# The residual placed in PSUM ahead of the expert products, and the last norm read from PSUM

## The chip, the cores and the metric

The kernel runs on one core of a Trainium2 chip. The metric is the device time of one execution in microseconds. A run gives the median of several executions; beside it one execution is profiled, and its trace gives every instruction's start and length.

## The reference

It is one layer of a transformer encoder over 512 tokens of width 1024, in float32. Attention of two kinds gives a mixed update, and the first norm gives `h`. What matters here is the second half of the layer:

```python
h = layer_norm(DN_ALPHA * h + mix, ln1_g, ln1_b)
ffn = peer_ffn(h, peer_w_q, peer_sub_keys, peer_u, peer_v)
gate = sigmoid(h @ ple_gate_w + ple_gate_b)
h = layer_norm(DN_ALPHA * h + ffn + gate * (p @ ple_w), ln2_g, ln2_b)

def peer_ffn(x, ...):            # per chunk of 128 tokens
    # idx, g: 8 heads x 16 experts of 16384, chosen by the best key sums, and their softmax
    hpre = einsum('td,ted->te', x, u_table[idx])
    act = g * gelu(hpre)
    return einsum('te,ted->td', act, v_table[idx])

def layer_norm(x, g, b):
    mu = mean(x); var = mean(square(x - mu))
    return (x - mu) * rsqrt(var + LN_EPS) * g + b
```

The layer ends with the last `layer_norm`, over the sum of the scaled `h`, the gate's part and the experts' part. The first two of these are the residual below.

## The kernel before

The 512 tokens are four chunks of 128. Chunk 0 (`NGC` is 1) is worked by gathering: for each of its 128 chosen experts POOL gathers a row of `u` or `v` per token into a buffer `gat`, and VectorE takes the dot product (line 1393) or adds the weighted row to `base[0]` (line 1404). Chunks 1 to 3 (`NDC` is 3, 384 tokens) are worked densely: the 16384 experts are 128 blocks of 128, and for each block TensorE multiplies the block's activations of 384 tokens with the block's 128 rows of `v` into PSUM.

For the dense chunks the sums of all blocks stand in PSUM from the first block to the last: `acc[c][hf]`, three chunks by two halves of 512 columns, six banks. Every operand is split into a high and a low part by the helper `split`: ScalarE copies the source to the high part (a cast to fp32r), VectorE subtracts it from the source for the low part. A block's products are three per bank (high by high, high by low, low by high), so 18 of 128x512, in `expert_out` (line 1419). The very first product into a bank has `start=True`, which overwrites what the bank held.

The residual is `base[c]`: for chunk 0 a tile of its own, for chunks 1 to 3 the tile `h[c]` itself, which the gate's last step (line 1232) overwrites with the scaled `h` plus the gate's part. This is done well before the loop.

Before the loop, "lead blocks" make the inputs of 100 of the 128 blocks: eight products of `u` by the tokens (`whole`), into the PSUM tile `mm`, or `hp` for the last two; then ScalarE's Gelu takes the sums out. These blocks and the gate's products are steps of the generator `pe_work`, one product each, which earlier stages advance as TensorE has time. What is left of it when the loop is near is run out in a fixed block just ahead of the loop. `mm` and `tr` (the sums of the routing weights, copied by ScalarE into `g_st`, line 1055) lie in the six banks that `acc` takes over.

The loop over the blocks has VectorE and SyncE in the order of the program (`manual_schedule`); the other engines are ordered by the scheduler of the language. In iteration `n` SyncE loads the rows of `v`, the routing weights `gt` and the activations `ge`; VectorE multiplies the latter two (line 1468); the two splits follow, then the 18 products. In the first 28 iterations `expert_in` makes the remaining blocks' inputs, with a 512 KB load of `raw` (line 116). The steps of chunk 0's gathers are spread over the iterations. The products of the last four blocks (124 to 127) are held back and run bank by bank, so that the banks complete one after the other.

After the loop all engines are ordered by the scheduler. For each chunk 1 to 3 VectorE adds `acc` to `base` half by half with the row sums as a by-product (line 1500); the mean comes from these sums, ScalarE squares the centred row with its sum as a by-product (line 151), and after the square root VectorE takes the reciprocal, four small steps that refine it (`rsqrt_refine`, lines 129 to 132), a centring pass with the gain (line 159) and a scaling pass with the bias (line 160). One store of 512 KB per chunk follows. Chunk 0 takes its mean and variance by `bn_stats` over two halves of `base[0]` instead.

Of the kernel before, what the change touches and what calls it, by code (L numbers as in the profile page):

```python
# [9 lines left out]
F32 = mybir.dt.float32  # L10
# [5 lines left out]
OP = mybir.AluOpType  # L16
# [3 lines left out]
D = 1024  # L20
# [7 lines left out]
EPS = 1e-5  # L28
# [45 lines left out]
def tile_encoder_layer(ctx: ExitStack, tc: tile.TileContext, A: dict, out: bass.AP):  # L74
    nc = tc.nc
# [1305 lines left out]
    psA = ctx.enter_context(tc.tile_pool(name="psA", bufs=1, space=PSUM, reuse_waits="tile"))  # L1381
    acc = [[psA.tile([128, 512], F32, name=f"acc{c}{hf}") for hf in range(2)] for c in range(NDC)]
    scr = pG.tile([128, D], F32, name="scr")

    def fetch_u(c, k):
        u = pG.tile([128, D], F32, name="gat", bufs=GATS)
# [27 lines left out]
    def expert_out(x, c, halves=(0, 1)):  # L1414
        n, ah, al, vh, vl = x
        cs = slice(c * 128, (c + 1) * 128)
        for i, (a, b) in enumerate(((ah, vh), (ah, vl), (al, vh))):
            for hf in halves:
                nc.tensor.matmul(acc[c][hf], a[:, cs], b[:, hf * 512:(hf + 1) * 512],  # L1419
                                 start=(n == 0 and i == 0), stop=(n == 127 and i == 2))  # L1420

    steps = list(gather_steps())
    late = []
# [1 line left out]
    with tc.manual_schedule(engines={nc.vector.engine, nc.scalar.engine, nc.tensor.engine, nc.sync.engine,  # L1425
                                     nc.gpsimd.engine}):
        gating = True
        gt_next = first_g
        v_next = {n: load_v(n) for n in (2, 3, 4)}
        for _ in pe_work:  # L1430
            pass
    done, spent = PRE, 0
    with tc.manual_schedule(engines={nc.vector.engine, nc.sync.engine}):
        for n, i in enumerate(order):
            if n % GB == 0:
                gt = gt_next
            if n < 128 - GB:
                for q in range(4):
                    if n % GB == (GB // 2 - 1 + q if n < KEPT + 128 - LEAD + 4 else GB - 2 + q // 2):
                        gt_next = load_g(n // GB * GB + GB, 3 - q if n < GB else q, gt_next, q == 0)  # L1440
            if n not in v_cut:
                raw = v_next.pop(n, None) or load_v(n)
            if n in v_cut:
                vh, vl = v_cut[n]
                ah = pO.tile([128, N_D], F32R, name="a_hi")
                al = pO.tile([128, N_D], F32R, name="a_lo")
            elif n in (124, 125):
                vh = wst.tile([128, D], F32R, name="whi")
                vl = wst.tile([128, D], F32R, name="wlo")
                a2 = wst.tile([128, 2, N_D], F32R, name="raw", bufs=3)  # L1450
                ah, al = a2[:, 0], a2[:, 1]
            else:
                if in_wst(n):
                    vh = wst.tile([128, D], F32R, name="whi")
                    vl = wst.tile([128, D], F32R, name="wlo")
                else:
                    vh = pP.tile([128, D], F32R, name="v_hi")
                    vl = pP.tile([128, D], F32R, name="v_lo")
                ah = pO.tile([128, N_D], F32R, name="a_hi")
                al = pO.tile([128, N_D], F32R, name="a_lo")  # L1460
            if 0 <= n + GE_AHEAD - (128 - SPILL) < SPILL:
                ge = pB.tile([128, N_U], F32, name="ge", bufs=GES)
                nc.sync.dma_start(ge, ge_dram[order[n + GE_AHEAD]])
                ge_t[order[n + GE_AHEAD]] = ge
            ge = ge_t.pop(i)
            a = gt[:, :, n % GB, :]
            dn = gt[:, N_S // GT:, n % GB, :]
            nc.vector.tensor_tensor(dn, dn, ge.rearrange("p (g t) -> p g t", t=GT), op=OP.mult)  # L1468
            if n not in v_cut:
                split(vh, vl, raw)  # L1470
            split(ah.rearrange("p (g t) -> p g t", t=GT), al.rearrange("p (g t) -> p g t", t=GT), a)
            late.append((n, ah, al, vh, vl))
            if n < 124:
                for c in range(NDC):
                    expert_out(late[0], c)
                late = []
            u = block_of_u(n)
            if u:
                expert_in(u)
            if n >= NO_GATHER:  # L1480
                spent += 1 if u else LATE
            upto = min(len(steps), PRE + math.ceil((len(steps) - PRE) * spent / (128 - (1 - LATE) * LEAD - 3 - NO_GATHER)))
            for f in steps[done:upto]:
                f()
            done = upto
# [5 lines left out]

    lg = row_bcast(pG, A["ln2_g"], "gat", GATS)
    lb = row_bcast(pG, A["ln2_b"], "gat", GATS)
    for c in range(4):
        fsum = None
        if c >= NGC:
            fsum = small.tile([128, 2], F32, name="fsum", bufs=2)
            for hf in range(2):
                hs = slice(hf * 512, (hf + 1) * 512)
                nc.vector.scalar_tensor_tensor(base[c][:, hs], base[c][:, hs], 1.0, acc[c - NGC][hf], op0=OP.mult,  # L1500
                                               op1=OP.add, accum_out=fsum[:, hf:hf + 1])
        layer_norm(base[c], lg, lb, fsum, scr)
        nc.sync.dma_start(out[c * 128:(c + 1) * 128, :], base[c])


# [85 lines left out]
```

## Time and profile before

| | |
|---|---|
| median of 3 runs | 1518.24 us (1515.72, 1518.24, 1519.31) |
| profiled execution, its own time | 1514.74 us |
| its span in the trace | 1512.7 us, so 2.0 us lie around it |
| granted TensorE clock, mean | 0.997 |
| TensorE busy | 1481.9 us, 98% |
| VectorE busy | 1302.4 us, 86% |
| ScalarE busy | 657.6 us, 43% |
| POOL busy | 571.9 us, 38% |

The trace's times are microseconds from the start of the span. PE is TensorE (PEld its weight loads), DVE VectorE, ACT ScalarE, SP SyncE; a q behind the name is an engine's instruction queue. `out<-in` names the tiles that an instruction writes and reads, and xN counts merged instructions. `base[1]` to `base[3]` are named `h` in the trace.

### The profile page before, as it was taken

Reading aid. Unit: us, or ns where it says so; the run is one execution under the profiler, and the core shown is the slowest. Engines: PE = TensorE matmul, PEld = TensorE weight load, DVE = VectorE, ACT = ScalarE, POOL = GpSimd, SP = SyncE. Lnnn points to the kernel's source line nnn. Section 1 sums busy time; section 2 is a strip of 40 time slices with the busy share of each in tenths; the row PEclk is TensorE's granted clock in tenths of the full one; section 3 lists DMA queues with packets and bytes.
Section 4 is the critical chain, followed back from the end, with each engine's and each line's share of the span. In section 5 each row is a group of like instructions: output and inputs, shape, how many; then the busy total and the mean of one; then the engine's idle time right before and its main releaser. Section 6 shows DMA issues by size and latency. Waiting matters only on the chain.

```text
span 1512.7 us, 23117 instructions
## 1 busy us (share of the span) xinstructions
PE 1481.9 (98%) x7757; PEld 1255.0 (83%) x7757; DVE 1302.4 (86%) x3020; ACT 657.6 (43%) x1224; POOL 571.9 (38%) x520
## 2 busy tenths in 40 slices
PE   8999999999999999999999999999999999999997
PEld 5788767788888889888988987888888888888885
DVE  7376785679989999899888978999999999999996
ACT  3355785333222566212765643444334333334342
POOL 1013110010015333455532434565555766666620
PEclk9999999999999999999999999999999999999999
DMA  7343240142279999999999999999999999999981
GB/s 250 98 116 95 84 126 29 42 143 84 89 226 335 341 401 379 416 408 412 400 407 375 388 384 382 411 410 416 414 413 411 412 411 409 412 411 409 412 323 76
DMA packets 194360, 459.90 MB, mean 304 GB/s; under 512 B 18241, under 2 KB 97985, under 8 KB 192706
## 3 DMA queue, kind: packets, MB, share of 16 engines
q1 hardware_dynamic: 121856, 214.60, 38.6%
q0 software_dynamic: 57984, 207.12, 34.8%
q10 hardware_dynamic: 14402, 36.71, 6.3%
q8 instruction: 61, 1.00, 0.2%
q14 instruction: 57, 0.47, 0.1%
HBM read 414.59 MB, written 40.89 MB: 301 GB/s over the span
## 4 chain that ended last, share of the span: by engine, by line
PE 69%; DVE 15%; DMA 8%; issue 4%; ACT 3%; POOL 1%; SPq 0%; DVEq 0%; POOLq 0%; ACTq 0%
PE acc L1419 33%; PE mm L1185 4%; PE mm L123 3%; PE hp L1185 3%; DMA wlo<-in_u_rows_dram,s_ix 3%; PE mm L125 3%; PE mm L124 3%; PE pj L123 3%; PE pj L124 3%; DMA whi<-in_u_rows_dram,s_ix 3%; PE tr L1043 3%; PE pj L125 3%; DVE oh_j L1081 2%; PE hp L123 2%; PE hp L125 2%
## 5 line engine op out<-in xcount | busy, mean ns | idle before, releaser
L1402 POOL DMA_INDIRECT gat<-in_v_rows_dram,i_sel x128 | 214.1, 1673 | 117.9 <-DVE base L1404 96.6
L1185 PE MATMUL mm<-whole,raw 128*128 128x256 f32 x848 | 190.9, 379 | 0.0
L104 ACT CAST whi<-raw 128x1024 fp32r<-128x1024 f32 (+4 forms) x117 | 117.3, 1004 | 160.6 <-DMA raw<-in_v_rows_dram 44.7
L1387 POOL DMA_INDIRECT gat<-in_u_rows_dram,i_sel x102 | 131.5, 1289 | 118.2 <-DVE hdot L1393 75.5
L1185 PEld LDWEIGHTS mm<-whole,raw 128*128 128x128 f32 x848 | 158.8, 190 | 20.4
L104 DVE TENSOR_TENSOR wlo<-raw,whi 128x1024 fp32r<-128x1024 f32 (+4 forms) x117 | 136.0, 1163 | 34.8 <-ACT whi L104 34.6
L1404 DVE SCALAR_TENSOR_TENSOR base<-gat,hdot,base 128x1024 f32<-128x1024 f32 x128 | 163.8, 1280 | 1.6
L1419 PE MATMUL acc<-v_hi,a_hi 128*128 128x512 f32 x480 | 149.5, 392 | 3.4 <-ACT a_hi L104 3.4
L1419 PE MATMUL acc<-v_lo,a_hi 128*128 128x512 f32 x480 | 149.0, 390 | 0.0
L1419 PE MATMUL acc<-v_hi,a_lo 128*128 128x512 f32 x480 | 148.8, 390 | 0.0
L104 ACT CAST v_hi<-v_raw 128x1024 fp32r<-128x1024 f32 x80 | 84.1, 1051 | 116.7 <-issue 49.1
L104 ACT CAST a_hi<-gt 128x384 fp32r<-128x384 f32 x126 | 64.6, 513 | 158.4 <-DVE gt L1468 99.3
L1098 POOL DMA_INDIRECT whi<-in_u_rows_dram,s_ix x51 | 57.7, 1131 | 199.6 <-DVE cand L946 133.5
L1393 DVE CUSTOM_DVE_ANT_0 scr<-gat,h 128x1024 f32<-128x1024 f32 x102 | 124.6, 1222 | 2.3
L1081 DVE TENSOR_SCALAR oh_j<-iota,eT 128x128 f32<-128x128 f32 x384 | 114.6, 372 | 0.0
L1419 PEld LDWEIGHTS acc<-v_lo,a_hi 128*128 128x128 f32 x480 | 90.2, 188 | 19.4 <-DVE v_lo L104 0.3
L1419 PEld LDWEIGHTS acc<-v_hi,a_lo 128*128 128x128 f32 x480 | 90.4, 188 | 19.1
L1419 PEld LDWEIGHTS acc<-v_hi,a_hi 128*128 128x128 f32 x480 | 88.5, 189 | 20.8 <-ACT a_hi L104 4.3
L104 DVE TENSOR_TENSOR v_lo<-v_raw,v_hi 128x1024 fp32r<-128x1024 f32 x80 | 97.4, 1217 | 7.8 <-ACT v_hi L104 7.7
L1043 PEld LDWEIGHTS tr<-oh_i,oh_j 128*128 128x128 f32 x768 | 93.5, 192 | 9.4 <-ACT g_st L1055 4.3
L1043 PE MATMUL tr<-oh_i,oh_j 128*128 128x128 f32 x768 | 95.9, 277 | 3.9 <-DVE oh_j L1081 2.1
L1098 POOL DMA_INDIRECT wlo<-in_u_rows_dram,s_ix x51 | 63.0, 1235 | 86.1 <-DVE s_dot L1100 45.8
(391 smaller groups left out, 3492.9 us busy)
## 6 DMA issues: line engine op xcount, KB each, us to landing
raw<-in_uT_dram SPq DMA_DIRECT2D x103, 512.0 KB, 7.2
v_raw<-in_v_rows_dram SPq DMA_DIRECT2D x82, 512.0 KB, 10.7
g_dram<-g_st ACTq DMA_DIRECT2D x12, 2048.0 KB, 10.5
gt<-g_dram SPq DMA_DIRECT2D x60, 384.0 KB, 12.9
raw<-in_v_rows_dram SPq DMA_DIRECT2D x44, 512.0 KB, 12.5
raw_u<-in_uT_dram SPq DMA_DIRECT2D x25, 512.0 KB, 6.8
ge_dram<-ge ACTq DMA_DIRECT2D x88, 128.0 KB, 6.7
ge<-ge_dram SPq DMA_DIRECT2D x88, 128.0 KB, 12.1
```

The costliest lines, as they stand in the source:

```text
L104: cut = nc.scalar.copy(hi, src), nc.vector.tensor_tensor(lo, src, r32(hi), op=OP.subtract)
L123: nc.tensor.matmul(ps, a[0], b[0], start=start, stop=False)
L125: nc.tensor.matmul(ps, a[1], b[0], start=False, stop=stop)
L1043: nc.tensor.matmul(ps[:, i * 128:(i + 1) * 128], oj[:, 4 * r + i, :], oi[:, 4 * r + i, :], start=True, stop=True)
L1081: nc.vector.tensor_scalar(oj[:, i], iota, eT[:, 1, t0 + i:t0 + i + 1], eT[:, 2, t0 + i:t0 + i + 1], op0=OP.is_equal, op1=OP.mult)
L1098: nc.gpsimd.indirect_dma_start(out=u[:], out_offset=None, in_=u_rows, in_offset=bass.IndirectOffsetOnAxis(ap=ix[:, k:k + 1], axis=0))
L1185: nc.tensor.matmul(ps[:, :N_U], raw[:, k], whole[:, k, :], start=(k == 0), stop=(k == 7))
L1387: nc.gpsimd.indirect_dma_start(out=u[:], out_offset=None, in_=u_rows, in_offset=bass.IndirectOffsetOnAxis(ap=i_sel[:, c, k:k + 1], axis=0))
L1393: nc.vector.tensor_tensor_reduce(scr, u, h[c], op0=OP.mult, op1=OP.add, accum_out=hdot[:, c, k:k + 1], scale=1.0, scalar=0.0)
L1402: nc.gpsimd.indirect_dma_start(out=u[:], out_offset=None, in_=v_rows, in_offset=bass.IndirectOffsetOnAxis(ap=i_sel[:, c, k:k + 1], axis=0))
L1404: nc.vector.scalar_tensor_tensor(base[c], u, hdot[:, c, k:k + 1], base[c], op0=OP.mult, op1=OP.add)
L1419: nc.tensor.matmul(acc[c][hf], a[:, cs], b[:, hf * 512:(hf + 1) * 512], start=(n == 0 and i == 0), stop=(n == 127 and i == 2))
```

## The change

Ahead of the loop, in its fixed block, `pe_work` is advanced by eight steps; then for each of the six banks a product of two slices of `hTh` (the transposed `h`, with no use for its value) is written with `start=True`, and ScalarE copies the residual of that chunk and half over it. The rest of `pe_work` follows, and the loop's products all add to what stands in the bank. The casts to the high parts of block 0's activations and of block 2's rows of `v` are ordered behind the last of these copies.

Behind the loop, chunk 0 is normed as before. For chunks 1 to 3 VectorE and SyncE follow a written order: `bn_stats` of each half straight from PSUM, the aggregate, the centring from PSUM into `base` by halves, the scaling, and then the next chunk's first statistics. For the last chunk the second half is centred after the first half is scaled and stored, and then scaled and stored by itself.

```diff
@@ -1381,6 +1381,14 @@
     psA = ctx.enter_context(tc.tile_pool(name="psA", bufs=1, space=PSUM, reuse_waits="tile"))
     acc = [[psA.tile([128, 512], F32, name=f"acc{c}{hf}") for hf in range(2)] for c in range(NDC)]
     scr = pG.tile([128, D], F32, name="scr")
+    halves = [slice(hf * 512, (hf + 1) * 512) for hf in range(2)]
+
+    def open_sums():
+        for c in range(NDC):
+            for hf, hs in enumerate(halves):
+                nc.tensor.matmul(acc[c][hf], hTh[:, 0, 0:128], hTh[:, 0, :], start=True, stop=False)
+                last_copy = nc.scalar.copy(acc[c][hf], base[NGC + c][:, hs])
+        return last_copy
 
     def fetch_u(c, k):
         u = pG.tile([128, D], F32, name="gat", bufs=GATS)
@@ -1417,7 +1425,7 @@
         for i, (a, b) in enumerate(((ah, vh), (ah, vl), (al, vh))):
             for hf in halves:
                 nc.tensor.matmul(acc[c][hf], a[:, cs], b[:, hf * 512:(hf + 1) * 512],
-                                 start=(n == 0 and i == 0), stop=(n == 127 and i == 2))
+                                 start=False, stop=(n == 127 and i == 2))
 
     steps = list(gather_steps())
     late = []
@@ -1427,6 +1435,9 @@
         gating = True
         gt_next = first_g
         v_next = {n: load_v(n) for n in (2, 3, 4)}
+        for _ in range(8):
+            next(pe_work)
+        opened = open_sums()
         for _ in pe_work:
             pass
     done, spent = PRE, 0
@@ -1467,8 +1478,14 @@
             dn = gt[:, N_S // GT:, n % GB, :]
             nc.vector.tensor_tensor(dn, dn, ge.rearrange("p (g t) -> p g t", t=GT), op=OP.mult)
             if n not in v_cut:
+                if n == 2:
+                    turned.append(opened)
                 split(vh, vl, raw)
+                turned.clear()
+            if n == 0:
+                turned.append(opened)
             split(ah.rearrange("p (g t) -> p g t", t=GT), al.rearrange("p (g t) -> p g t", t=GT), a)
+            turned.clear()
             late.append((n, ah, al, vh, vl))
             if n < 124:
                 for c in range(NDC):
@@ -1491,16 +1508,48 @@
 
     lg = row_bcast(pG, A["ln2_g"], "gat", GATS)
     lb = row_bcast(pG, A["ln2_b"], "gat", GATS)
-    for c in range(4):
-        fsum = None
-        if c >= NGC:
-            fsum = small.tile([128, 2], F32, name="fsum", bufs=2)
-            for hf in range(2):
-                hs = slice(hf * 512, (hf + 1) * 512)
-                nc.vector.scalar_tensor_tensor(base[c][:, hs], base[c][:, hs], 1.0, acc[c - NGC][hf], op0=OP.mult,
-                                               op1=OP.add, accum_out=fsum[:, hf:hf + 1])
-        layer_norm(base[c], lg, lb, fsum, scr)
+    for c in range(NGC):
+        layer_norm(base[c], lg, lb)
         nc.sync.dma_start(out[c * 128:(c + 1) * 128, :], base[c])
+
+    stats = [small.tile([128, 2, 6], F32, name=f"st_{c}", bufs=1) for c in range(NDC)]
+
+    def stat(c, hf):
+        nc.vector.bn_stats(stats[c][:, hf, :], acc[c][hf])
+
+    with tc.manual_schedule(engines={nc.vector.engine, nc.sync.engine}):
+        stat(0, 0)
+        for c in range(NDC):
+            r = base[NGC + c]
+            o = out[(NGC + c) * 128:(NGC + c + 1) * 128]
+            ys = small.tile([128, 8], F32, name="ln_y")
+            mu = small.tile([128, 2], F32, name="ln_mu")
+            ve, sd, y0, y, t = (ys[:, i:i + 1] for i in range(5))
+
+            def centre(hf):
+                hs = halves[hf]
+                nc.vector.scalar_tensor_tensor(r[:, hs], acc[c][hf], mu[:, 0:1], lg[:, hs], op0=OP.subtract, op1=OP.mult)
+
+            def scale(hs):
+                nc.vector.scalar_tensor_tensor(r[:, hs], r[:, hs], y, lb[:, hs], op0=OP.mult, op1=OP.add)
+                nc.sync.dma_start(o[:, hs], r[:, hs])
+
+            stat(c, 1)
+            nc.vector.bn_aggr(mu, stats[c])
+            nc.vector.tensor_scalar(ve, mu[:, 1:2], EPS, None, op0=OP.add)
+            nc.scalar.sqrt(sd, ve)
+            centre(0)
+            if c < NDC - 1:
+                centre(1)
+            nc.vector.reciprocal(y0, sd)
+            rsqrt_refine(y, y0, ve, t)
+            if c < NDC - 1:
+                scale(slice(0, D))
+                stat(c + 1, 0)
+            else:
+                scale(halves[0])
+                centre(1)
+                scale(halves[1])
 
 
 # ---- launch: one core; host code only lays the arrays out ----
```

## Rows read from the trace of the kernel before

**Rows 1.** The page, part 1: busy time, share of the span, instructions.

```profile
PE 1481.9 (98%) x7757; PEld 1255.0 (83%) x7757; DVE 1302.4 (86%) x3020; ACT 657.6 (43%) x1224; POOL 571.9 (38%) x520
```

**Rows 2.** Chain of waits, 855 to 960 us: start, us, what.

```profile
893.89 12.30 PE acc L1419 x54
...
906.22 1.07 ACT v_hi L104
...
913.29 10.17 DMA raw<-in_uT_dram
```

**Rows 3.** Timeline of TensorE: start, us, operation, [idle before, what ended it].

```profile
886.82 3.62 PE L1185 MATMUL hp<-whole,raw 128*128 128x256 f32 x16
...
925.94 1.22 PE L1419 MATMUL acc<-v_hi,a_hi 128*128 128x512 f32 x2 [3.44 <-ACT a_hi L104]
...
929.23 0.63 PE L1419 MATMUL acc<-v_lo,a_hi 128*128 128x512 f32 x2
```

**Rows 4.** Windows: engines' busy time, then granted clock, DMA share, GB/s.

```profile
893.50:898.00 4.50, 4.50 (x21) 3.71 (x20) 1.56 (x2) 2.79 (x4) 3.04 (x3) 1.00 0.97 286
...
922.00:926.00 4.00, 0.56 (x4) 0.13 (x2) 0.49 (x1) 2.40 (x3) 1.02 (x2) 0.93 1.03 422
...
926.00:936.00 10.00, 10.00 (x40) 8.07 (x41) 9.37 (x15) 3.67 (x5) 3.19 (x3) 0.86 0.89 323
```

**Rows 5.** Chain of waits, 1380 us to the end.

```profile
1379.85 113.78 PE acc L1419 x500
...
1493.66 1.91 DVE h L1500 x6
...
1507.69 1.28 DVE h L160
```

**Rows 6.** Timeline of TensorE and VectorE, 1502.3 us to the end.

```profile
1502.55 0.39 PE L1419 MATMUL acc<-v_hi,a_lo 128*128 128x512 f32 x1
...
1503.04 0.68 DVE L1500 SCALAR_TENSOR_TENSOR h<-h,acc 128x512 f32<-128x512 f32 x1
...
1506.73 0.15 DVE L154 RECIPROCAL ln_y<-ln_y 128x1 f32<-128x1 f32 x1
```

**Rows 7.** Timeline of ScalarE at the seam.

```profile
884.00 0.58 ACT L1055 COPY g_st<-tr 128x512 f32<-128x512 f32 x1 [0.31 <-PE tr L1043]
...
886.89 0.65 ACT L1167 ACTIVATE ge<-mm 128x256 f32<-128x256 f32 x2
...
890.75 0.50 ACT L104 CAST a_hi<-gt 128x384 fp32r<-128x384 f32 x1
...
894.95 1.05 ACT L104 CAST v_hi<-v_raw 128x1024 fp32r<-128x1024 f32 x1 [0.63 <-DMA g_dram<-g_st]
```

**Rows 8.** Waits of POOL, 860 to 900 us: total, times, longest.

```profile
POOL gat L1387 <- PE hp L1185: 19.6, 1, 19.6
```

**Rows 9.** Timeline of VectorE, the first norm of the kernel.

```profile
4.62 1.29 DVE L337 BATCH_NORM_STATS2 ln_st<-h 128x6 f32<-128x512 f32 x2 [4.62 <-DMA h<-in_x_dram]
5.94 0.21 DVE L339 BATCH_NORM_AGGREGATE ln_mu<-ln_st 128x2 f32<-128x12 f32 x1
6.18 0.15 DVE L341 TENSOR_SCALAR ln_y<-ln_mu 128x1 f32<-128x1 f32 x1
```

**Rows 10.** Timeline of VectorE, chunk 0's last norm inside the loop.

```profile
1472.87 0.15 DVE L144 TENSOR_SCALAR ln_y<-ln_mu 128x1 f32<-128x1 f32 x1
1472.94 1.27 DVE L157 SCALAR_TENSOR_TENSOR base<-base,ln_mu,gat 128x1024 f32<-128x1024 f32 x1
1474.13 0.16 DVE L154 RECIPROCAL ln_y<-ln_y 128x1 f32<-128x1 f32 x1
...
1487.33 1.22 DVE L104 TENSOR_TENSOR wlo<-v_raw,whi 128x1024 fp32r<-128x1024 f32 x1 [6.18 <-ACT whi L104]
```

**Rows 11.** DMA issues: KB each, median us from issue to landing.

```profile
out_dram<-h SPq DMA_DIRECT2D x3, 512.0 KB, 2.6
...
ple_dram<-pl SPq DMA_DIRECT2D x4, 256.0 KB, 2.3
```

## The prediction, made before the change was run

> **What bounds the kernel now.** I read the page first. TensorE is busy 98% of the span, VectorE 86% [rows 1], but that is a mean over stages, and the change touches two short ones: the seam where the loop over the expert blocks begins, and the last 20 us. So I read the chain of waits around each, then the order of the engines there.
>
> *The seam.* The products of the loop start as soon as TensorE is done with the last two lead blocks; the chain runs from those products through ScalarE's cast of `v_hi` (its buffer is given back by the products at 906.2), through VectorE to a 512 KB load of `raw`, issued at 913.29 and landed 10.17 us later, and from there to the next product [rows 2]. TensorE sits idle for 3.44 us until 925.94 [rows 3]. Behind that wait its first products are slow: from 925.94 to 929.23, in four rows of two, eight products take 3.29 us. [...] From there on the chain is TensorE without a gap; its last 113.78 us before the tail are 500 products at 0.228 [rows 5].
>
> *The tail.* The chain leaves TensorE at 1493.66, when the first chunk's sums are complete, and stays on VectorE (with ScalarE's squares between) up to the last pass, which starts at 1507.69 and takes 1.28 [rows 5]. TensorE ends at 1502.55 + 0.39 = 1502.94, and VectorE takes up the last half at 1503.04 [rows 6], but it had only just come free. So the tail is VectorE's: 15.31 us from 1493.66 to 1508.97, then the last store.
>
> **The change, part by part.**
>
> *Six opening products.* They are 128x512 products of the loop's kind, 6 x 0.228 = 1.37 us of TensorE that were not there. In the code the eight steps ahead of them are the last four products of lead block 97 and the first four of block 98, so they stand in the middle of the 16 rows that begin at 886.82 [rows 3], at about 888.7. ScalarE left the last bank that they write at 886.89 + 0.65 = 887.54 [rows 7]; I cost the wait for the banks at nothing. If that cover went, it would be the time by which ScalarE is late, 0 to 1 us.
>
> *Six copies into PSUM.* No row shows a copy to PSUM. The nearest is the copy of 128x512 out of PSUM, 0.58 [rows 7]. At most 6 x 0.58 = 3.5 us. They begin at about 889.1, when the first opening product is complete, and end by 892.6. ScalarE has a hole there: between 887.54 and the cast of `a_hi` at 890.75 only one Gelu stands. The Gelu of block 98 and the cast for block 0 now come behind the copies, the cast at about 893. The products need that cast at 893.89 + 1.37 = 895.26 [rows 2], so it stays hidden with more than a microsecond to spare. Below nothing is excluded: the copies start nothing earlier.
>
> *What the 1.37 us do next.* Everything at the seam moves: the first product from 893.9 to 895.3, the return of the `v_hi` buffer, the cast, VectorE's `v_lo` and with it the load of `raw`. POOL moves too: its gathers wait for the last lead product (19.6 us of waiting) [rows 8], so they restart 1.37 us later. Against this stands the DMA. [...] But just at the restart it is not full: 893.5 to 898 moves 286 GB/s, where 922 to 926, in the wait, moves 422 [rows 4]. [...] Bounds: all of it passes to the end, +1.37; or `raw` lands when it did, the wait shrinks to about 2.1 us, and at best the slow products go too, -1.47. Between ends this far apart I go by the row that is nearest, the chain, which ties the load to the products, and take half of the delay, +0.7.
>
> *The tail on VectorE.* Per chunk, from the first statistics pass. Two `bn_stats` to the aggregate, 5.94 - 4.62 = 1.32; to the add of EPS, 0.24 [rows 9]; to the centring pass 0.07; the centring 1.19 as one pass (1474.13 - 1472.94), 1.22 as two halves; reciprocal and four steps up to the scaling pass, 1507.69 - 1506.73 = 0.96; the scaling, 1.20 like the centring [rows 5, 6, 10]. Sum 5.01, and two such chunks 10.02. ScalarE's square root stands under the centring, which is longer than it; if that cover went it would cost under half a microsecond per chunk. The last chunk: 1.32 + 0.24 + 0.07 + half a centring 0.61 + 0.96 + half a scaling 0.61, then centring 0.68 and scaling 0.68 one behind the other, as the second reads the first: 5.17. In all 15.19 against 15.31, a gain of 0.12. The sums don't hold it up: the last half is needed at 1493.66 + 10.02 + 0.61 = 1504.3 and complete at 1502.94. What is removed is one addition pass per half and the square on ScalarE; what comes for it is one statistics pass per half. They cost the same, so only the stretches in which VectorE waited for the square are won, and the old order had mostly filled these with the next chunk's additions.
>
> The unseen operations are `bn_stats` from PSUM and the centring from PSUM. From SBUF two statistics passes take 1.29 [rows 9], 0.61 up to the second if that one takes 0.68; an addition that reads PSUM takes 0.68 too [rows 6]. I price both at that. Bounds: 0.03 more or less for each of twelve passes, plus or minus 0.4 over the tail. [...]
>
> *The last store by halves.* 512 KB to the output take 2.6 us from issue to landing, a 256 KB store 2.3 [rows 11]. The first half goes out while VectorE works on the second, so the end gains 0.3; bounds 0 and 0.6 (twice that, if the transfer alone scaled). [...]
>
> **Sum.** +0.7 - 0.1 - 0.3 = +0.3. The profiled execution took 1514.74 us, its span 1512.7 and 2.0 around it; with the change 1515.0. That execution was 3.5 us quicker than the median of the runs shown, 1518.24, so for the median 1518.5. A change of 0.2%, about what a measurement of this kernel can tell from none, is 3.0 us.
>
> **Rivals.**
> [...]
> 2. *Chunk 0's norm slides behind the loop (slower).* This norm is not in a fixed order; its passes stand between the loop's at 1472.87 to 1474.13 [rows 10]. If, with the new fixed block behind it, they come behind the loop's last cast, their about 5.0 us (the sum of a chunk above) fall into the tail, where VectorE is the bound: 1518.5 + 5.0 = 1523.5. It decides where they stand behind the block that waits from 1481 to 1487 (VectorE idles 6.18 us there [rows 10], so anything ahead of that is free). Against it: the program order of norm and loop is unchanged.
> 3. *A cast gets ahead of the copies.* Only the value cast of block 2 and the gate cast of block 0 are ordered behind the copies. Were block 3's cast ahead, the copies would stand behind a cast that can't start before 894.95, when a store of `g_st` lands [rows 7]. The copies would end at about 899.1, the products of block 0 about 3 us later than before, and with the same tail 1518.24 + 3.1 - 0.4 = 1520.9. Against it: block 3 comes behind block 2.
> 4. *The change does nothing at either end.* The opening is absorbed with the clock as before, and each of the twelve passes over PSUM costs 0.03 more than a row shows: 1518.24 + 0 - 0.1 + 0.4 - 0.3 = 1518.2. [...] Against it: the equal 0.68 us. [...]
>
> **How the numbers follow.** The likeliest, half to all of the delay passing and a small gain behind, has 0.58; rival 1 has 0.15, rival 2 0.08, rival 3 0.07, rival 4 0.12. The likeliest one's own range is 1518.24 + 0 - 0.5 - 0.6 = 1517.1 to 1518.24 + 1.37 + 0.3 = 1519.9; with the lower bound of the opening the low end is 1515.6. The runs shown lie between 1515.72 and 1519.31, so a median can lie a microsecond away by itself. 1515.4 to 1521.0 takes in rivals 1, 3 and 4 and leaves out rival 2 and what I have not seen. Faster by over 0.2% needs all bounds at their best and luck besides: 0.10. Slower comes from rival 2 and a part of rival 3: 0.11. Same: 0.79.
>
> **What will show it.** Right, if the six products and copies stand at about 888.7 to 892.6, the first product of the loop at about 895.3, TensorE again waits for the load of `raw` and goes on between 925.9 and 927.3, VectorE spends about 15.2 us from its first statistics pass to the last scaling, and the last store begins about half a microsecond sooner behind TensorE's last product. Wrong, if TensorE waits at the copies, if the wait at 922 vanishes or doubles, if chunk 0's norm stands behind the loop, or if the passes over PSUM take 0.75 us rather than 0.68.

## The result and the profile after

| | before | after |
|---|---|---|
| median, timed side by side, 6 runs each | 1516.64 us (1514.20 to 1519.31) | 1530.52 us (1528.03 to 1532.92) |
| ratio | | 1.0089 [1.0079, 1.0100] |
| span of the profiled execution | 1512.7 us | 1528.2 us |
| granted TensorE clock, mean | 0.997 | 0.995 |

The change makes the kernel 0.9% slower, about 13.9 us. The prediction said 1518.5 and at most 1521.0.

Part 1 of the page of the changed kernel, which answers to [rows 1]:

```profile
PE 1493.3 (98%) x7763; PEld 1257.9 (82%) x7763; DVE 1304.2 (85%) x3015; ACT 656.4 (43%) x1224; POOL 564.8 (37%) x520
```

TensorE has six products more and is busy 11.4 us longer, in a span that is 15.5 us longer. Six products are 1.4 us. So 10 us of the loss lie in TensorE's work that was there before, and the ends are not the only place to look. I first looked at the two places that the prediction names.

The timeline of TensorE in the changed kernel, at the seam and later, answers to [rows 3]:

```profile
888.11 1.74 PE L1389 MATMUL acc<-hTh 128*128 128x512 f32 x6
...
894.68 0.81 PE L1427 MATMUL acc<-whi,a_hi 128*128 128x512 f32 x2
...
914.76 1.22 PE L1427 MATMUL acc<-v_hi,a_hi 128*128 128x512 f32 x2 [2.54 <-ACT a_hi L104]
...
930.68 0.73 PE L1427 MATMUL acc<-v_hi,a_hi 128*128 128x512 f32 x2 [1.84 <-ACT a_hi L104]
...
1172.74 0.72 PE L1427 MATMUL acc<-whi,a_hi 128*128 128x512 f32 x2 [2.62 <-ACT a_hi L104]
```

And the timeline of ScalarE there, which answers to [rows 7]:

```profile
888.73 3.18 ACT L1390 COPY acc<-h 128x512 f32<-128x512 f32 x6 [1.44 <-PE acc L1389]
891.85 0.51 ACT L104 CAST a_hi<-gt 128x384 fp32r<-128x384 f32 x1
895.18 1.05 ACT L104 CAST v_hi<-v_raw 128x1024 fp32r<-128x1024 f32 x1 [2.82 <-DMA g_dram<-g_st]
```

The opening itself goes as predicted: the six products without a wait, the copies behind them, the cast of `a_hi` done 2.3 us before the first product of the loop needs it, and that product 1.14 us later than before (894.68 against 893.54). But before had one wait of 3.4 us in the loop, and after has three of 7.0 us together, at 914, 930 and 1172. The last lies 280 us from anything that the change edits.

What ended last, by the chain of waits of the changed kernel, 975 to 1528 us:

```profile
1132.70 1.14 DVE scr L1401
...
1138.50 12.69 DMA raw<-in_v_rows_dram
...
1156.57 14.58 DMA raw<-in_v_rows_dram
...
1172.74 336.65 PE acc L1427 x1453
```

And the matching piece in the chain of the kernel before, 1100 to 1513 us:

```profile
1127.09 366.54 PE acc L1419 x1615
```

There are two things to see. Before 1172 the chain has left TensorE: from 1095 on it stands on VectorE's splits and dot products (the first row shown is one of these), and then on two loads of `raw`. And behind it TensorE runs without a gap to the tail, as in [rows 5], but at 336.65 / 1453 = 0.2317 us a product, where the last 500 before took 0.228 and the matching piece of before 366.54 / 1615 = 0.2270.

The windows view of the changed kernel, 1200 to 1400 us (columns as in [rows 4]), shows the same at full granted clock:

```profile
1200.00:1400.00 200.00, 200.00 (x870) 163.08 (x869) 188.53 (x222) 72.59 (x97) 126.59 (x76) 1.00 1.04 403
```

and the kernel before:

```profile
1200.00:1400.00 200.00, 200.00 (x884) 165.62 (x883) 190.22 (x224) 73.70 (x98) 130.26 (x77) 1.00 1.04 411
```

Before has 884 products in the same 200 us where after has 870, and both are busy throughout at a granted clock of 1.00. So this loss is neither waiting nor clock. The timeline of TensorE shows whose products are slow. The first rows of four blocks' products (each block is 18 products, and from block 37 on every second block holds its rows of `v` in `whi` and `wlo`, the others in `v_hi` and `v_lo`):

```profile
1294.61 0.63 PE L1427 MATMUL acc<-v_hi,a_hi 128*128 128x512 f32 x2
...
1298.70 0.62 PE L1427 MATMUL acc<-whi,a_hi 128*128 128x512 f32 x2
...
1302.90 0.63 PE L1427 MATMUL acc<-v_hi,a_hi 128*128 128x512 f32 x2
...
1306.99 0.62 PE L1427 MATMUL acc<-whi,a_hi 128*128 128x512 f32 x2
```

First rows of three blocks in the timeline of TensorE before:

```profile
1465.60 0.61 PE L1419 MATMUL acc<-whi,a_hi 128*128 128x512 f32 x2
...
1469.68 0.61 PE L1419 MATMUL acc<-v_hi,a_hi 128*128 128x512 f32 x2
...
1473.76 0.61 PE L1419 MATMUL acc<-whi,a_hi 128*128 128x512 f32 x2
```

A block from `v_hi` lasts 4.09 us after the change, a block from `whi` 4.20; before, both last 4.08. The mean from start to start over blocks 52 to 121 is 232.6 ns for products that stream `whi`, 233.3 for `wlo`, and 226.6 to 226.7 for all four tiles before.

From the starts of the blocks in both traces, the difference after minus before builds up so:

| at the start of block | 0 | 9 | 37 | 44 | 50 | 123 | end of span |
|---|---|---|---|---|---|---|---|
| us later than before | 1.1 | 5.4 | 5.8 | 6.3 | 11.1 | 15.7 | 15.5 |

That is 1.1 for the opening, 4.3 at the seam, some 0.9 up to block 44, about 4.8 around blocks 44 to 50 (the wait at 1172 and slow products behind it, at a granted clock of 0.75 from 1172 to 1176 us and 0.82 from 1176 to 1180), 4.6 of slow pace from there on, and 0.1 given back at the end.

The tail on VectorE, in the timeline of the changed kernel, answers to [rows 5, 6]:

```profile
1509.41 1.29 DVE L1518 BATCH_NORM_STATS2 st<-acc 128x6 f32<-128x512 f32 x2 [0.74 <-PE acc L1427]
...
1511.06 1.40 DVE L1531 SCALAR_TENSOR_TENSOR h<-acc,ln_mu,gat 128x512 f32<-128x512 f32 x2
...
1513.34 1.29 DVE L1534 SCALAR_TENSOR_TENSOR h<-h,ln_y,gat 128x1024 f32<-128x1024 f32 x1
...
1523.57 0.75 DVE L1531 SCALAR_TENSOR_TENSOR h<-acc,ln_mu,gat 128x512 f32<-128x512 f32 x1
1524.36 0.75 DVE L1534 SCALAR_TENSOR_TENSOR h<-h,ln_y,gat 128x512 f32<-128x512 f32 x1
```

From 1509.41 to 1524.36 + 0.75 = 1525.11 it takes 15.70 us (predicted 15.19, before 15.31). The span ends 3.1 us behind it; before it ended 3.7 behind [rows 5]. So the store by halves gave 0.6, the tail lost 0.4, and the span ends 9.48 us behind TensorE's last product instead of 9.72.

**What the rows leave.** The instructions that are slow, or late, are not those that were edited. One thing that the diff does reaches all of them: it drops the tile `fsum` (two buffers of 32 bytes a partition) and adds `st_0` to `st_2` (three of 64 bytes) in the pool `small`. This pool stands at the head of the left side of SBUF, and by the program's allocation everything larger behind it on that side moves on by 3 x 64 - 2 x 32 = 128 bytes. Tiles on the right side keep their places:

```
byte in the partition                before   after
hTh (left)                            34816   34944
whi, first buffer (left)              79872   80000
gat, end of the eighth buffer (left) 176128  176256
g_st, begin (right)                  176128  176128
```

Before, the buffers of `gat` end just where `g_st` begins. After, the last of them laps over it by 128 bytes.

### The profile page after: what moved, and what is told of

Same layout as the page of the kernel before. It is cut to its first block, busy times and chain, and to the rows that moved or that the text cites. A ratio compares the mean times of both kernels' runs of the same rounds, so it can differ in the third digit from the quotient of the medians.

```text
span 1528.2 us, 23123 instructions
## 1 busy us (share of the span) xinstructions
PE 1493.3 (98%) x7763; PEld 1257.9 (82%) x7763; DVE 1304.2 (85%) x3015; ACT 656.4 (43%) x1224; POOL 564.8 (37%) x520
## 4 chain that ended last, share of the span: by engine, by line
PE 78%; DVE 11%; DMA 5%; issue 3%; ACT 3%; SPq 0%; POOL 0%; DVEq 0%; ACTq 0%; POOLq 0%
PE acc L1427 30%; PE mm L1185 14%; PE hp L1185 5%; PE tr L1043 5%; PE mm L123 3%; PE mm L124 3%; PE mm L125 3%; PE pj L123 3%; PE pj L124 3%; PE pj L125 3%; DMA raw<-in_v_rows_dram 2%; DMA wlo<-in_u_rows_dram,s_ix 2%; PE hp L123 2%; PE hp L125 1%; PE hp L124 1%
## 5 line engine op out<-in xcount | busy, mean ns | idle before, releaser
L1410 POOL DMA_INDIRECT gat<-in_v_rows_dram,i_sel x128 | 210.7, 1646 | 130.3 <-DVE base L1412 109.0
L1081 DVE TENSOR_SCALAR oh_j<-iota,eT 128x128 f32<-128x128 f32 x384 | 109.8, 357 | 0.0
L104 DVE TENSOR_TENSOR a_lo<-gt,a_hi 128x384 fp32r<-128x384 f32 x126 | 69.8, 554 | 30.2 <-ACT a_hi L104 29.1
```

What stands on the lines that cost most here:

```text
L104: cut = nc.scalar.copy(hi, src), nc.vector.tensor_tensor(lo, src, r32(hi), op=OP.subtract)
L1081: nc.vector.tensor_scalar(oj[:, i], iota, eT[:, 1, t0 + i:t0 + i + 1], eT[:, 2, t0 + i:t0 + i + 1], op0=OP.is_equal, op1=OP.mult)
L1410: nc.gpsimd.indirect_dma_start(out=u[:], out_offset=None, in_=v_rows, in_offset=bass.IndirectOffsetOnAxis(ap=i_sel[:, c, k:k + 1], axis=0))
```

## The experiments

The pool `small` begins with an unused tile of `GAP_SMALL` columns of 4 bytes, so 32 columns move what lies behind it by 128 bytes and add no instruction. `GAP_SUMS` is such a tile behind `whi`, `wlo` and the tiles of chunk 0's routing, ahead of `gat`. The order of the instructions on each engine is that of the unmoved kernel wherever only places are changed.

| run | edit | median us | its before | ratio |
|---|---|---|---|---|
| e1 | after, 128 bytes back | 1516.83 | 1517.16 | 1.0004 [0.9994, 1.0015] |
| e2 | before, 128 bytes on | 1528.76 | 1517.16 | 1.0075 [1.0057, 1.0092] |
| e3 | before with the opening | 1517.56 | 1517.16 | 1.0005 [0.9993, 1.0017] |
| e4 | before with the end | 1516.91 | 1517.16 | 1.0004 [0.9991, 1.0018] |
| e5 | before, `gat` 128 on | 1519.60 | 1515.06 | 1.0026 [1.0014, 1.0038] |
| e6 | before, `raw`, `whi`, `wlo` 128 on | 1526.18 | 1515.06 | 1.0069 [1.0052, 1.0087] |
| e7 | the same, 64 on | 1523.20 | 1515.06 | 1.0055 [1.0032, 1.0079] |
| e8 | the same, 256 on | 1517.22 | 1515.06 | 1.0016 [0.9996, 1.0035] |
| e9 | before, `whi`, `wlo` 128 on | 1526.33 | 1516.54 | 1.0060 [1.0037, 1.0082] |
| e10 | before, `raw` 128 on, `whi`, `wlo` 256 on | 1518.23 | 1516.54 | 1.0006 [0.9992, 1.0020] |
| e11 | before, one buffer of `v_hi` off by 128 | 1519.44 | 1516.54 | 1.0017 [1.0001, 1.0032] |
| e12 | after, 128 on (256 in all) | 1519.09 | 1516.54 | 1.0011 [0.9998, 1.0023] |

Beside the medians I use the length of the loop in the profiled execution, from its first product to the end of its last. It leaves out the stages ahead of the loop: the loop's first product starts between 893.5 and 899.4 us in these executions, a spread of 6 us that does not follow the edits. The length is 609.4 us before and 624.0 after.

### The places or the operations (e1 to e4)

The two theories are that the places of the tiles cost the time (P), or that the change's own operations do (O): the products and copies at the seam and what they delay. e1 keeps every operation of the change and takes back the move; e2 is before with the move alone.

```diff
 # e1, on the changed kernel
-GAP_SMALL, ... = 96, ...
+GAP_SMALL, ... = 64, ...
 # e2, on the kernel before
-GAP_SMALL, ... = 96, ...
+GAP_SMALL, ... = 128, ...
```

> The change with the padding tile at the head of the pool of small tiles cut by 128 bytes, which is what the new statistics tiles add, so that every large tile lies where it lay before; the instructions and their order are those of the change. Theory P (the loss comes from where the tiles lie): the products that read whi and wlo are back at 0.227 us each, POOL's third early gather is again at 873, TensorE's second wait near block 44 is gone, and the time is 1516.6 + 1.1 of the opening - 0.3 of the end = 1517.4, at most 1518.5. Theory O (the loss comes from the six products and copies and from the order of ScalarE's casts that they bring about): nothing changes, 1530.5.

> The kernel before with the same padding tile grown by 128 bytes, so that every large tile of the left side lies where the change puts it; nothing else differs. Theory P: most of the loss appears without the change: whi and wlo products at 0.233, some 5.5 us over the second half of the loop, and the lost early gathers with 4 to 8 us at the seam and near block 44; 1526 to 1530. Theory O: 1516.6, within 2 us.

e1 is no longer slower, with a loop of 609.1 us; e2 is, with a loop of 622.4. The whole of the loss that can be measured follows the 128 bytes, and O falls. The windows view of e1 has before's 884 products again:

```profile
1200.00:1400.00 200.00, 200.00 (x884) 165.59 (x883) 190.50 (x225) 73.19 (x98) 128.32 (x77) 1.00 1.04 411
```

e3 and e4 do one part each, at before's places. In e3 the old end stays, with its addition of the residual made harmless, since the opening has added it already; the places are before's, as `fsum` stays. e4 has the old start and the new end; the sums of chunks 1 to 3 get no residual there, so it leaves out one term of the layer.

```diff
 # e3, on the kernel before: open_sums() and the order of the casts as in the change, and
-                nc.vector.scalar_tensor_tensor(base[c][:, hs], base[c][:, hs], 1.0, acc[c - NGC][hf], op0=OP.mult,
+                nc.vector.scalar_tensor_tensor(base[c][:, hs], base[c][:, hs], 0.0, acc[c - NGC][hf], op0=OP.mult,
 # e4, on the changed kernel: GAP_SMALL 64, without open_sums() and what is ordered behind it, and
-                                 start=False, stop=(n == 127 and i == 2))
+                                 start=(n == 0 and i == 0), stop=(n == 127 and i == 2))
```

> The opening alone (six products, six copies, the ordering of two casts), with the end of the kernel before, where the addition pass multiplies the residual by zero since the sums hold it already; tiles lie as before. Theory P: 1516.6 + 0 to 1.4 = 1516.6 to 1518.0, the first product of the loop 1.1 us later. Theory O: 1530 less at most half a microsecond.

> The end alone (statistics and centring from PSUM, last chunk by halves), with the loop of the kernel before and the tiles moved back by 128 bytes; nothing is copied into PSUM, so the residual of the three dense chunks is left out of the sums. Both theories: 1516.6 - 0.3 (the trace of the change shows 0.24 less between TensorE's last product and the end of the span), so 1516.0 to 1516.7. If the end is what costs, more than 1518.

Neither part can be told from before, in the median or in the loop (609.4 and 608.9). From TensorE's last product to the end of the span e3 takes 9.75 us and e4 9.50, so the end does gain its 0.2 us, a tenth of what a measurement resolves. All the traces agree on it: with the new end this stretch takes 9.48 to 9.51 us (after, e1, e4, e12), with the old one 9.67 to 9.86 (the other ten).

### Which tile's place (e5 to e8)

The move does two things that could be told apart: `gat` laps over `g_st`, and `raw`, `whi` and `wlo` lie elsewhere. The theories P1 and P2 of these expectations share the loss out between the two in different ways. e5 moves `gat` alone, e6 to e8 the other tiles alone; these take `base_0` and the tiles of chunk 0's routing along, up to `GAP_SUMS`.

```diff
 # e5
-    scr = pG.tile([128, D], F32, name="scr")
+    scr = pG.tile([128, D + 32], F32, name="scr")[:, :D]
 # e6 (e7: 16 and 112; e8: 64 and 64)
-GAP_SMALL, GAP_EDGE, GAP_SUMS, ... = 96, 216, 128, ...
+GAP_SMALL, GAP_EDGE, GAP_SUMS, ... = 96, 216, 96, ...
-    hTl = keep.tile([128, 8, T], F32R, name="hTl")
+    hTl = keep.tile([128, 8 * T + 32], F32R, name="hTl")[:, :8 * T].rearrange("p (k t) -> p k t", t=T)
```

> The kernel before with the buffers gat alone moved by 128 bytes (scr made that much longer); whi and wlo stay. The last gat buffer now reaches 128 bytes into the place of a g_st buffer, as it does in the change. Theory P1 (this overlap holds the gathers back until the last store from g_st has read it out, and the waits of TensorE come from that): only one gather starts before 890, not three; the waits at the seam and near block 44 appear, 5 to 9 us, 1521 to 1526, and all products stay at 0.227. Theory P2 (the whole loss is the pace of whi and wlo products and what hangs on it): 1516.9, three early gathers.

> The kernel before with raw, whi, wlo (and the residual of chunk 0 behind them) moved by 128 bytes, and everything from the activations on back in its place, so that gat overlaps nothing. Theory P1: whi and wlo products at 0.233, three early gathers, no wait near block 44, and 5 to 6 us from the pace: 1522 to 1523. Theory P2: the whole loss, 1528.8.

> As the run with 128 bytes, with 64. If what counts is that a row of 512 elements of whi or wlo no longer starts where it did (at a multiple of 2048 bytes), the pace is 0.233 again and the time 1522 to 1523; if the loss grows with the distance, 0.230 and about 1519.8; if 64 bytes are a step that does no harm, 0.227 and 1516.9.

> As the run with 128 bytes, with 256. Any departure counts alike: 0.233 and 1522 to 1523. Graded with the distance: 0.239 and about 1528. Only steps below 256 do harm: 0.227 and 1516.9.

Both count. With the overlap alone (e5) the loop is 612.4 us, 3.0 longer, at before's pace per product (226.5 to 226.8 ns), and the first nine blocks take 47.67 us instead of 44.93. The first gathers of chunk 0's rows on POOL in e5:

```profile
873.10 2.21 POOL L1387 DMA_INDIRECT gat<-in_u_rows_dram,i_sel  x1 [0.30 <-issue]
900.65 0.95 POOL L1387 DMA_INDIRECT gat<-in_u_rows_dram,i_sel  x1 [25.34 <-issue]
```

and in e1, whose `gat` ends where `g_st` begins:

```profile
872.11 2.21 POOL L1395 DMA_INDIRECT gat<-in_u_rows_dram,i_sel  x1 [0.30 <-issue]
874.63 0.98 POOL L1395 DMA_INDIRECT gat<-in_u_rows_dram,i_sel  x1 [0.30 <-ACT oh_i L1073]
876.98 1.28 POOL L1395 DMA_INDIRECT gat<-in_u_rows_dram,i_sel  x1 [1.37 <-DMA g_dram<-g_st]
899.29 0.94 POOL L1395 DMA_INDIRECT gat<-in_u_rows_dram,i_sel  x1 [21.03 <-PE hp L1185]
```

Without the overlap three gathers go out ahead of POOL's long wait, with it one. The row puts the 25 us down to nothing in particular, but the trace's semaphores tell the reason. In e5 POOL's instruction queue stands from 871.77 to 899.85 us in one instruction that waits for two semaphores; one of them tells of the last store from `g_st`, issued at 889.34, and takes its last step at 899.82. In the changed kernel the same two times are 895.13 and 895.10. By the program's allocation the second gather goes into just the buffer that ends last, the one that laps over `g_st`. So it is held until the store has read that tile out, and the third gather stands behind it. The two gathers that were early now fall into the first blocks, where the DMA's share is 1.03 in the wait already before [rows 4]. What that costs is seen in all fourteen traces: the first nine blocks take 46.9 to 49.2 us in the four kernels with the overlap (after, e2, e5, e12) and 44.0 to 46.0 in the ten without.

With the weights' tiles alone moved (e6) the loop is 616.8 us, 7.4 longer, the three early gathers stand, TensorE has one wait of 3.5 us in the loop as before, and the products from `whi` and `wlo` have the pace of the changed kernel (870 products of all kinds from 1200 to 1400 us, as there). So this is the larger part. 64 bytes (e7) cost about as much in the median, though less in the loop (614.1 us), and with 229.3 and 230.8 ns the products of `whi` and `wlo` are about half as far from before's pace (those of `v_hi` and `v_lo`, which did not move, rise to 228.7 and 231.0). 256 bytes (e8) cost nothing that can be told: 608.8 us of loop, before's pace (226.5 to 226.9 ns).

One thing fell here: that the wait near block 44 comes from the overlap alone. Behind 990 us e5 has no wait of TensorE; the two kernels with both effects wait there (after 2.6 us in one wait, e2 3.1 in three), and with the weights' tiles alone it is 0.2 at most (e7; e3, at before's places, has 0.5). In these traces, one execution of each kernel, waits of over half a microsecond there take both, and no run splits it further.

### Which read or write, and a second place (e9 to e12)

`raw` is written by the loads, `whi` and `wlo` are written by ScalarE and VectorE and streamed by TensorE. Theory R (read) holds that the place of `whi` and `wlo`, which TensorE streams, sets the pace, theory W (write) that of `raw`, where the loads land. In e6 to e10 the residual of chunk 0 (`base_0`) moves along with `whi` and `wlo`; e11 moves neither.

```diff
 # e9, with GAP_SUMS 96
-        hi = wst.tile([128] + shape, F32R, name="whi")
+        wst.tile([128, 32], F32, name="pad", bufs=1); hi = wst.tile([128] + shape, F32R, name="whi")
 # e10: the same pad, hTl as in e6, GAP_SUMS 64
 # e11
-                    vh = pP.tile([128, D], F32R, name="v_hi")
+                    vh = pP.tile([128, D + 32], F32R, name="v_hi")[:, :D]
 # e12, on the changed kernel
-GAP_SMALL, ... = 96, ...
+GAP_SMALL, ... = 128, ...
```

> The kernel before with whi and wlo moved by 128 bytes and raw left in place (the residual of chunk 0 and its dot products move along). Theory R (the place of the operand that TensorE streams counts): whi and wlo products at 0.233 over the second half of the loop, products of v_hi and v_lo at 0.227 to 0.228. Theory W (the place counts where the loads land and the casts read, raw): all at 0.227, and the time as before.

> The counterpart: raw moved by 128 bytes, whi and wlo by 256, which did no harm. Theory R: all products at 0.227, within 2 us of before. Theory W: whi and wlo products at 0.233 and 1520 or more.

> The kernel before with the first of the two v_hi buffers moved by 256 bytes and the second by 128; v_lo and all else stay. Theory R: products that stream the second v_hi buffer take 0.233, those of the first 0.227, so every other block that uses v_hi has 12 of 18 products 6 ns longer: about 0.07 us in a quarter to a half of the blocks, 2 to 4 us in all. If the place matters only for whi and wlo (their neighbours in the left half of the memory), all at 0.227 and the time as before.

> The change with the padding tile grown by 128 bytes, so that the large tiles of the left side lie 256 bytes from their places in the kernel before. Theory R: products at 0.227 again, but gat still reaches into g_st, so the gathers start late: the loss of the run that moved gat alone, 1517 + 4 = 1519 to 1522. If the distance from the old place is what counts, as slow as the change or slower, 1530.

R holds against W. In e9, with `raw` in its place, the products of the moved tiles are slow (all products from 1200 to 1400 us are 871, where before has 884), and of the others only the first three behind each such block (231 to 233 ns; the changed kernel and e6 have the same three); first rows of three blocks from its timeline of TensorE:

```profile
1295.44 0.63 PE L1419 MATMUL acc<-v_hi,a_hi 128*128 128x512 f32 x2
...
1299.54 0.62 PE L1419 MATMUL acc<-whi,a_hi 128*128 128x512 f32 x2
...
1303.73 0.63 PE L1419 MATMUL acc<-v_hi,a_hi 128*128 128x512 f32 x2
```

4.10 and 4.19 us, where before has 4.08 for both. In e10, with `raw` where e6 had it but `whi` and `wlo` 256 bytes on, all are at before's pace (226.5 to 226.9 ns).

e11 does the same to the other side of SBUF, with `base_0` in its place: its `v_hi` has two buffers, and with the pad one lies 256 bytes from its old place, the other 128. The blocks from the second are slow, one block in four; from its timeline of TensorE:

```profile
1294.01 0.62 PE L1419 MATMUL acc<-v_hi,a_hi 128*128 128x512 f32 x2
...
1298.09 0.62 PE L1419 MATMUL acc<-whi,a_hi 128*128 128x512 f32 x2
...
1302.17 0.62 PE L1419 MATMUL acc<-v_hi,a_hi 128*128 128x512 f32 x2
...
1306.33 0.63 PE L1419 MATMUL acc<-whi,a_hi 128*128 128x512 f32 x2
...
1310.43 0.62 PE L1419 MATMUL acc<-v_hi,a_hi 128*128 128x512 f32 x2
```

4.08, 4.08, 4.16, 4.10. The expected 2 to 4 us came (2.6 by the ratio, whose interval reaches from 0.2 to 4.9). What I had not expected: within the slow block the products of `v_lo`, which keeps its place, are slow too (231 to 235 ns), and so are the first three of the next block (231 to 233).

e12 puts the change another 128 bytes on, so that the pace should return and the overlap stay. The pace does return (226.5 to 226.8 ns; 884 products in 1200 to 1400 us), the loop is 611.6 us, and on POOL one early gather is left:

```profile
871.89 2.21 POOL L1395 DMA_INDIRECT gat<-in_u_rows_dram,i_sel  x1 [0.30 <-issue]
899.33 0.94 POOL L1395 DMA_INDIRECT gat<-in_u_rows_dram,i_sel  x1 [25.23 <-issue]
```

Its ratio lies 0.8% below that of the changed kernel, with the same operations in the same order: two kernels that differ in one constant. What the overlap costs here can't be told by the ratio, which includes 1; the cost of the overlap by itself rests on e5's ratio and on the length of the first nine blocks (46.92 us in e12).

The change at before's places (e1) and its end alone (e4) are not faster than before by anything that can be measured.

## Why the prediction was wrong

**The step that failed** is the list in "The change, part by part": what it has the change remove and add are instructions, waits and stores, and no tiles. It put the cost of everything between the seam and the tail at nothing, without a reason. `fsum` and `st_0` to `st_2` are in the diff, and I priced the passes that write them and not the place that they take. None of the rivals has it either, and the lower and upper bounds are made of the same terms. What the runs showed in its place: two small tiles more or less move the large ones by 128 bytes, and this move alone, without the change, makes the loop 13.0 us longer (e2, 1.0075 [1.0057, 1.0092]), while the change without the move costs nothing that can be measured (e1, 1.0004 [0.9994, 1.0015]). So 1518.5 is the forecast for a kernel that moves nothing; that kernel is e1, and it measured 1516.83, beside 1517.16 for before.

**The pace.** "From there on the chain is TensorE without a gap" was read rightly [rows 5], and what follows from it was not drawn: with TensorE the bound over 128 blocks, 0.11 us in every second block from 37 to 123 and 0.01 in the others make 44 x 0.11 + 43 x 0.01 = 5.3 us. The prediction's price of 0.228 a product was used for the six new ones only and taken as fixed for the other 2304.

**The seam.** Opening products and copies stand in the order that the text gave, at 888.1 to 891.9, some 0.6 us ahead of the times forecast, and the cast 1.2 us ahead; TensorE did not wait at the banks; by the chain of waits the six products took 1.39 us. The copies took 0.53 us each (3.18 for six), where 0.58 was taken. Half of the 1.37 was to pass on to the end, the 0.7 of the sum: the author's choice between two bounds, and no run shows such a half. With the places undone the whole can't be told from nothing: the loops of e1 and e3 (609.1 and 609.4 us) are as long as before's (609.4), and both ratios include 1. The wait of 3.44 us [rows 3] became two in the changed kernel, 2.54 and 1.84, which end at 914.76 and 930.68 and not between 925.9 and 927.3. The size of this wait is no measure of the opening: in the ten kernels without the overlap the longest there lies between 1.8 and 3.6 us, with the opening and without. The first nine blocks tell more, and they follow the gathers that came late: after takes 49.18 us, e2, without the opening, 47.94, and e1, with it, 44.39. The 1.47 of the lower bound is the eight products behind the wait, 3.29 us [rows 3], less 8 x 0.228 = 1.82. No run shows that a shorter wait gives all of it back: the first eight took 3.44 and 3.46 us behind the waits of 2.54 and 1.84 in the changed kernel (granted clock 0.50 from 915 to 917 us and 0.67 from 931 to 933), and 2.36 behind one of 2.19 in e1. The split of the 1.37 us had a weak ground besides: "at the restart it is not full" went by 286 GB/s, but the DMA's share in the same row is 0.97 [rows 4].

**The tail.** The new term was mis-sized. Predicted were 15.19 us, measured 15.70. Passes of 512 columns with two tensors and a scalar from a tile take 0.74 to 0.75 us, where 0.68 and, behind another, 0.61 were taken: 0.12 and 0.10 us in the first two chunks (5.13 and 5.11 against 5.01), 0.29 in the last (5.46 against 5.17). The 0.68 row was an addition with a fixed scalar 1.0 [rows 6], another form. The pass from PSUM and the one from SBUF are equally long (0.75 and 0.75 in the last two rows of the tail), and the statistics from PSUM take 1.29 for two, as from SBUF [rows 9]. So the tail lost 0.4, where it was to gain 0.12, with passes that take the same time over PSUM and SBUF. The 0.03 us a pass of the bounds was an estimate of the author's that no run shows; the passes of 512 columns took 0.06 to 0.07 more than the 0.68.

**The store.** 0.6 was gained, not 0.3: the upper bound. From VectorE's last pass to the end of the span it was 3.7 us before and 3.1 after. Tail and store together were to gain 0.42 and gained 0.24: two misses of opposite sign.

**The rivals.** Chunk 0's norm stayed in the loop (rival 2), no cast went ahead of the copies (rival 3: `a_hi` at 891.85 stands right behind them, and the `v_hi` cast that waits for the store of `g_st` comes after it). Rival 3's price of 3.1 does not follow from its own terms: copies that end at 899.1 and a cast of 0.50 behind them put the first product near 899.6, 6 us later than before and not 3. What the operations alone did is e1: its interval holds the forecast's +0.3 us and rival 4's 0, which can't be told apart, and leaves out a gain of 1.9, which the lower bound of the opening (-1.47) and 0.4 of tail and store would make (rival 1). Of the signs listed as wrong, "0.75 us rather than 0.68" came; "the wait at 922 vanishes or doubles" came only in that the wait split into two, 4.4 us together.

**What stays open** is why 128 bytes slow the products, and why the overlap and the slow pace together make waits near block 44 (and in e2 ahead of it) that neither makes alone.

## What to carry to other kernels

Read a diff for the tiles that it adds and drops, not only for its instructions: a few bytes at the head of a pool move everything behind them, and here that cost 0.9% while the edit itself cost nothing that could be measured. Before judging a change, run it once with a pad that puts the large tiles back; a loss that stays is the change's own. And where instructions that nobody edited get slower at full clock and without waits, compare the addresses first.

## What the runs showed of the hardware

The pace of TensorE's 128x512 products at full granted clock (1.00 from 1200 to 1400 us) went with where the streamed tiles lie. Mean start to start over blocks 52 to 121, `whi` / `wlo`:

| moved by | ns | run |
|---|---|---|
| 0 | 226.7 / 226.6 | before |
| 64 bytes | 229.3 / 230.8 | e7 |
| 128 bytes | 232.6 / 233.3 | after (e2, e6, e9 alike) |
| 256 bytes | 226.5 to 226.9 | e8, e10, e12 |

The first buffer of `whi` began at 39 x 2048 bytes; 256 bytes on it is as fast, so the multiple of 2048 is not what matters. The places of `whi`, `wlo` and `v_hi` that were fast are all multiples of 256 bytes and the slow ones are not; that is a pattern of the few places tried, not a rule that was tested. That tiles which did not move slow down beside the moved ones (`v_hi` and `v_lo` at 228.7 and 231.0 ns in e7, `v_lo` at 231 to 235 in e11) says that it is not the read of the one tile by itself; whether it is a meeting with the writes of the next block's tiles was not tried.
